# The input stage of a hybrid decoder layer: where the meta tokens' norm runs, and in which order tokens and weights are loaded

## The chip, the cores and the metric

The kernel runs on one core of a Trainium2 chip. A core has a matrix engine (TensorE, PE in the profile), a vector engine (VectorE, DVE), a scalar engine (ScalarE, ACT), GpSimd (POOL) and a sync engine (SyncE, SP). They run side by side and meet through semaphores. SyncE and ScalarE each have a queue from which DMA transfers are issued. The metric is the device time of one execution in microseconds (us); the median over runs is taken.

## The reference

A layer of a decoder trunk in float32, for 1024 tokens of width 1024 with 16 meta tokens put in front. Cut to what matters here:

```python
h = jnp.concatenate([meta, x], axis=1)          # 16 + 1024 tokens
h = layer_norm(h, in_ln_g, in_ln_b)             # the input norm
z = h @ w_in + b_in                             # q | k | v | conv input | gates
a = swa_sink_attention(q, k, v, sinks, ...)     # window 128, 16 meta keys seen by all
c = silu(layer_norm(causal_dwconv(c_val * sigmoid(c_gate), conv_dw, conv_dw_b)))
mixed = sigmoid(g_attn) * (a @ w_attn_proj) + sigmoid(g_conv) * (c @ w_conv_proj)
h = layer_norm(ALPHA * h + mixed @ w_out, ln1_g, ln1_b)
u, g = split(causal_dwconv(h @ ffn_w_up, ffn_dw, ffn_dw_b))
out = layer_norm(ALPHA * h + (gelu(g) * u) @ ffn_w_down, ln2_g, ln2_b)
```

The input norm is `(x - mean) * rsqrt(var + eps) * g + b` for each token; nothing of the big product `h @ w_in` can begin before the first tokens are normed.

## The kernel before, in words

Float32 precision is kept by splitting each operand into a rounded high part and the low rest, and by adding three products (high·high, high·low, low·high) of the faster matmul type. After the input stage the kernel works through the products z, attention and convolution (interleaved), the projections, the FFN's up and down products, and the last norm.

**The input stage.** Tokens come as eight tiles of 128 (`xt[0]` to `xt[7]`) and the meta tokens as one tile `xm`, which holds the 16 tokens twice (partitions 0 to 15 and 16 to 31). Groups of tiles share one norm: group 0 is the meta tile, group 1 is x0 and x1, group 2 is x2, x3 and x4, group 3 is x5, x6 and x7. For each group:

- `stat` (L440, L441): VectorE takes mean and variance of each tile, two halves of 512 and one step that joins them;
- `table` (L464): ScalarE takes the approximate reciprocal square root of the variance;
- `newton` (L470 to L473): VectorE improves it by one Newton step in three operations, and a fourth gives minus mean times root;
- `norm` (L483 on VectorE or L485 on ScalarE): each tile is scaled and shifted, in two halves of 512;
- `turns` (L503): TensorE transposes the normed tiles, eight chunks `k` of 128 features each;
- `scaled` (L509): ScalarE copies the transposed chunk out of PSUM with the norm's gain and offset; `high` and `low` (L516 to L523) split it;
- `z_first` (L557 with the unsplit operands, L560 with the split ones): TensorE's products with the first three weight tiles (k, v and the first q tile).

The first products for tokens 0 to 271 need the meta tile, x0 and x1 together. For chunks 4 to 7 a transposition and a product of L557 take turns on TensorE, with a copy by ScalarE between them.

**What sets the order.** In this stage the order on VectorE, ScalarE and TensorE is the order in which the calls stand from L573 on: the helpers `dv`, `ac` and `pe` chain each instruction to the one before it on its engine. DMA issues have ranks (`with rank(...)`), by which a list scheduler places them. SyncE's queue before is: the meta tokens (twice), x0, x1, the column constants `coll` and `colr`, the first two weight tiles, x2, the third weight tile, x3, x4, x5, x6, x7, a table, the gain rows. A transfer's semaphore is one of eight that are used in turn, so an issue can wait for the eighth transfer before it. After the input stage the scheduler, which plans with its own estimate of times, chooses the order of the instructions of all engines.

At the start, twenty matmuls on a constant (L575) keep TensorE busy until there is something to do. `later` keeps each tile's mean and root for the residual, which is formed long after (L293, L294).

Of the kernel before, what the change touches and what calls it, by code (L numbers as in the profile page):

```python
# [23 lines left out]
F = mybir.dt.float32  # L24
R = mybir.dt.float32r
AF = mybir.ActivationFunctionType
# [3 lines left out]
P = 128  # L30
D = 1024
KC = D // P
NMETA = 16
# [42 lines left out]
RK_TURN, RK_SPLIT, RK_EVAC, RK_START, RK_QKV, RK_RESID, RK_ATT = 450, 500, 600, 1000, 10000, 20000, 30000  # L76
# [36 lines left out]
def tile_hybrid_layer(  # L113
# [3 lines left out]
    nc = tc.nc  # L117
# [5 lines left out]
    def load(o, i):  # L123
        return nc.sync.dma_start(out=o, in_=i)

    def store(o, i):

        return nc.scalar.dma_start(out=o, in_=i)
# [4 lines left out]
    def after(ins, first):  # L133

        tc.add_manual_dep(ins.ins, first.ins.name, mybir.DependencyInfo(
            mybir.DependencyClass.NoSync, mybir.DependencyReason.SCHED_ONLY), reason="order of work")

    @contextmanager
    def rank(p):

        saved = tc.cur_priority
        tc.cur_priority = p
        yield
        tc.cur_priority = saved
# [36 lines left out]
    sp = start.enter_context(tc.tile_pool(name="start", bufs=1, side="right", reuse_waits="tile"))  # L181

    eps = const2.tile([P, 1], F, name="eps")
# [8 lines left out]
    xm = sp.tile([P, D], F, name="xm")  # L192
    with rank(0):
        nc.gpsimd.memset(xm[32:64], 0.0)
        nc.gpsimd.memset(xm[64:96], 0.0)
    with rank(5):
        for i in range(2):
            load(xm[i * NMETA:(i + 1) * NMETA], meta_tokens)
    xt = []

    def load_x(j):
# [98 lines left out]
    def wraw(shape):  # L300
        return wraw_p.tile(shape, F, name="wr", tag="wr")

    def split(raw, hi, lo, behind=None):
        ins = nc.scalar.copy(hi, raw)  # L304
        if behind is not None:
            after(ins, behind)
        return nc.vector.tensor_tensor(lo, raw, f32(hi), OP.subtract)  # L307

    def chunks(t):
        return [t[:, o:o + D].rearrange("p (k c) -> p k c", k=KC) for o in W_AT]  # L310

    def wsp(dtype=R):
        return wsp_p.tile([P, W_LEN], dtype, name="w", tag="w")
# [8 lines left out]
    def weights(shape, fill):  # L322
        fills[0] += 1
        n = fills[0]
        own = n == 3
        raw = OB[:, 0:D].rearrange("p (k c) -> p k c", k=KC) if own else wraw(shape)
        with rank({1: 14, 2: 13, 3: 16, 4: 23}.get(n, RK_SPLIT)):
            last_fill.append(fill(raw))
        hi, lo = chunks(sp.tile([P, W_LEN], R, name="w3") if own else wsp())
        if n <= 3:  # L330
            return hi, lo, raw
        with rank(RK_SPLIT):
            last_split.append(split(raw, hi, lo))
            if n == 7:
                after(last_split[-1], cin_done[-1])
        return hi, lo
# [22 lines left out]
    def z_tile(fill, groups, evac, wt=None):  # L359
        wt = wt or weights([P, KC, P], fill)  # L360
        return [z_group(wt, g, a, b, evac) for g, (a, b) in enumerate(groups)]
# [63 lines left out]
    tokens = [(-1,), (0, 1), (2, 3, 4), (5, 6, 7)]  # L425
    norms, xns, later = {}, {}, []

    def src_of(j):
        return (xt[j], P) if j >= 0 else (xm[:2 * NMETA], 2 * NMETA)

    def stat(t, *js):

        J = len(tokens[t])
        if t not in norms:
            norms[t] = [sp.tile([P, J, 2], F, name=f"mv{t}")] + [sp.tile([P, J], F, name=f"{n}{t}") for n in "trm"]
        for j in js:
            x_, n = src_of(j)
            st_ = small.tile([P, 2, 6], F, name="st")
            for i in range(2):
                dv(V.bn_stats(st_[:n, i], x_[:, i * 512:(i + 1) * 512]))  # L440
            dv(V.bn_aggr(norms[t][0][:n, tokens[t].index(j)], st_[:n].rearrange("p a b -> p (a b)")))  # L441
# [4 lines left out]
        dv(V.tensor_scalar(nsink, sink, -1.0, None, OP.mult))  # L446

    half_st = {}

    def half_stat(t, j, i):  # L450

        if t not in norms:
            norms[t] = [sp.tile([P, len(tokens[t]), 2], F, name=f"mv{t}")] + [
                sp.tile([P, len(tokens[t])], F, name=f"{n}{t}") for n in "trm"]
        if i == 0:
            half_st[j] = small.tile([P, 2, 6], F, name="st")
        dv(V.bn_stats(half_st[j][:, i], xt[j][:, i * 512:(i + 1) * 512]))
        if i == 1:
            dv(V.bn_aggr(norms[t][0][:, tokens[t].index(j)], half_st[j][:, :].rearrange("p a b -> p (a b)")))

    def table(t):
        mv, t_, r_, m_ = norms[t]
        n = src_of(tokens[t][0])[1]
        ac(nc.scalar.activation(r_[:n], mv[:n, :, 1], AF.Abs_reciprocal_sqrt, bias=eps[:n], scale=1.0))  # L464

    def newton(t):
        n = src_of(tokens[t][0])[1]
        mv, t_, r_, m_ = (x_[:n] for x_ in norms[t])
        stt = V.scalar_tensor_tensor
        dv(stt(t_, mv[:, :, 1], EPS, r_, OP.add, OP.mult))  # L470
        dv(stt(t_, t_, -0.5, r_, OP.mult, OP.mult))
        dv(stt(r_, t_, 1.5, r_, OP.add, OP.mult))
        dv(stt(m_, mv[:, :, 0], -1.0, r_, OP.mult, OP.mult))  # L473

    def norm(t, j, on_dve):
        x_, n = src_of(j)
        i = tokens[t].index(j)
        mv, t_, r_, m_ = norms[t]
        xns[j] = sp.tile([P, D], F, name="xn", tag="xn", bufs=4) if j >= 0 else xm
        to = xns[j] if j >= 0 else xm[96:]  # L480
        for a in range(0, D, 512):
            if on_dve:
                dv(V.tensor_scalar(to[:, a:a + 512], x_[:, a:a + 512], r_[:n, i:i + 1], m_[:n, i:i + 1], OP.mult, OP.add))  # L483
            else:
                ac(nc.scalar.activation(to[:, a:a + 512], x_[:, a:a + 512], AF.Identity, bias=m_[:n, i:i + 1],  # L485
                                        scale=r_[:n, i:i + 1]))
        later.append((x_, mv[:n, i, 0:1], r_[:n, i:i + 1], n, j))

    GT = [(-1, 0, 1), (2, 3, 4), (5, 6, 7)]
    turned, tms = {}, {}  # L490
# [34 lines left out]
    def parts(g, *ks):  # L525
        for k in ks:
            high(g, k, on_dve=True)
            low(g, k)

    first = [weights([P, KC, P], in_cols(m)) for m in (4, 5, 0)]  # L530
    evacs0 = [k_evac, v_evac, q_evac(0)]

    def whigh(i):
        ac(nc.scalar.copy(first[i][0], first[i][2]))
# [11 lines left out]
    def z_first(g, tiles, *ks, raw=False):  # L546

        for i in tiles:
            a, b = span(i, g)
            if ks[0] == 0:  # L550
                sums0[i] = pat.tile([P, 512], F, name="ps_z", tag="mm", bufs=3)[:, :b - a]
        for k in ks:
            for i in tiles:
                a, b = span(i, g)
                hi, lo, w = first[i]
                if raw:
                    pe(nc.tensor.matmul(sums0[i], w[:, k], tms[g, k][:, a - HG[g][0]:], start=k == 0, stop=k == KC - 1))  # L557
                    continue
                for j, (w, hl) in enumerate(((lo, 0), (hi, 0), (hi, 1))):
                    ins = nc.tensor.matmul(sums0[i], w[:, k], h0(k, hl, a, b), start=k + j == 0,  # L560
                                           stop=k == KC - 1 and j == 2)
                    if j == 0:
                        pe(ins)
                    pe_done.append(ins)
# [10 lines left out]
        pe(nc.tensor.matmul(warm[:, :P], ones, ones, start=True, stop=True))  # L575
    stat(0, -1)
    table(0)
    stat(1, 0)
    newton(0)
    norm(0, -1, False)  # L580
    stat(1, 1)
    table(1)
    newton(1)
    norm(1, 0, True)
    norm(1, 1, False)
    scales()
    turns(0, 0, 1, 2, 3)
# [10 lines left out]
    evac(0, 0)  # L598
    stat(2, 3)
    stat(2, 4)  # L600
    whigh(1)
    table(2)
    z_first(0, (1,), *range(8), raw=True)
    evac(0, 1)
    newton(2)
# [64 lines left out]

    tc.cur_priority = RK_QKV + 3000
    wt_c1 = weights([P, KC, P], in_cols(11))
    tc.cur_priority = RK_RESID
    for src, mu, rs, n, j in later:
# [19 lines left out]
    bias = ap.tile([P, NH, 272], F, name="bias")  # L694
# [832 lines left out]
    for c in range(FC):  # L1527
        V4, X, Z, Y = (pup.tile([P, 1024], F, name=n, tag=n) for n in ("pw", "px", "pz", "py"))
        passes = ((1,), (0,)) if c == 0 else ((0, 1),)
        for subs in passes:  # L1530
            last = subs == passes[-1]
            w_next = iter(range(7))
            a, b = SUB[subs[0]][0], SUB[subs[-1]][1]
# [314 lines left out]
```

## Time and profile before

| what | us |
|---|---|
| median of 3 runs (range) | 1264.09 (1262.23 to 1264.21) |
| profiled execution, its own time | 1263.24 |
| its span in the trace | 1261.5 |
| TensorE busy, whole span | 1247.8 (99%) |
| VectorE busy | 1076.5 (85%) |
| ScalarE busy | 595.0 (47%) |

How to read the rows in the next section: times count from the start of the span. A row of the timeline has start, busy time, engine, line, operation, `out<-in`, shape and count, and in brackets how long the engine stood idle before it and what ended that. SPq and ACTq are the DMA queues of SyncE and ScalarE. A row of the stretches has, for a stretch of time, its length, each engine's busy time and count of instructions, the granted clock of TensorE (1.00 is full speed), the share of the DMA engines and GB/s. The chain is followed back from the last instruction: each piece is what the next one waited for.

### The profile page before, as it was taken

The numbers are of one execution on the slowest core, as the hardware profiler recorded it, in microseconds if no ns is written. First come the engines' busy times: TensorE is split into PE (matmuls) and PEld (weight loads), VectorE is DVE, ScalarE is ACT, GpSimd is POOL, SyncE is SP. The second block draws the span as 40 slices with busy tenths as digits, with TensorE's granted clock in tenths as the row PEclk, the third lists the DMA queues.
The fourth block names the chain that finished last, engine by engine and source line by source line (L and its number), as shares of the span: only waits on it lengthen the run. The fifth ranks groups of instructions, "written<-read, shape, count | busy, mean of one in ns | idle before, by whom it ended". The sixth has DMA issues, their size and how long they took to land.

```text
span 1261.5 us, 23038 instructions
## 1 busy us (share of the span) xinstructions
PE 1247.8 (99%) x9186; PEld 1181.3 (94%) x9186; DVE 1076.5 (85%) x1858; ACT 595.0 (47%) x1100; POOL 8.0 (1%) x9
## 2 busy tenths in 40 slices
PE   8999999999999999999999999999999999999997
PEld 7999999999999999788999999999999998888886
DVE  7888999999978677448999999998989977996697
ACT  7532345655474233335665555554455544445330
POOL 0000000001000000000000000000000000000000
PEclk9999999999999999999999999999999999999999
DMA  6375543332256564222245546453454567998712
GB/s 254 105 256 145 170 120 97 106 93 85 72 155 169 164 166 124 84 85 82 68 157 196 196 171 216 160 209 135 157 205 165 192 225 252 392 353 329 271 63 84
DMA packets 98701, 212.19 MB, mean 168 GB/s; under 512 B 11411, under 2 KB 38611, under 8 KB 98338
## 3 DMA queue, kind: packets, MB, share of 16 engines
q1 hardware_dynamic: 84474, 199.64, 47.3%
q10 hardware_dynamic: 14120, 11.08, 2.8%
q8 instruction: 72, 1.18, 0.4%
q14 instruction: 35, 0.29, 0.1%
HBM read 150.29 MB, written 62.70 MB: 169 GB/s over the span
## 4 chain that ended last, share of the span: by engine, by line
PE 96%; DVE 2%; ACT 1%; DMA 0%; issue 0%; SPq 0%; DVEq 0%; ACTq 0%
PE px L1549 15%; PE py L1549 10%; PE ps_x L1694 9%; PE ps_z L342 8%; PE ps_z L345 8%; PE ps_z L346 8%; PE ps_z L1694 7%; PE pw L1549 5%; PE pz L1549 5%; PE ps_p L346 2%; PE ps_p L345 2%; PE ps_p L342 2%; PE ps_w L346 2%; PE ps_w L342 2%; PE ps_w L345 2%; PE ps_z L560 2%
## 5 line engine op out<-in xcount | busy, mean ns | idle before, releaser
L342 PE MATMUL ps_z<-RHO,w 128*128 128x256 f32 (+2 forms) x864 | 243.4, 282 | 0.0
L345 PE MATMUL ps_z<-RHO,w 128*128 128x256 f32 (+2 forms) x864 | 242.2, 280 | 0.0
L346 PE MATMUL ps_z<-RHC,w 128*128 128x256 f32 (+2 forms) x864 | 242.2, 280 | 0.0
L342 PEld LDWEIGHTS ps_z<-RHO,w 128*128 128x128 f32 x864 | 162.5, 188 | 1.2 <-ACT FA L709 0.7
L345 PEld LDWEIGHTS ps_z<-RHO,w 128*128 128x128 f32 x864 | 162.5, 188 | 0.5
L346 PEld LDWEIGHTS ps_z<-RHC,w 128*128 128x128 f32 x864 | 162.7, 188 | 0.2
L729 DVE SCALAR_TENSOR_TENSOR FA<-cin,cdw,FA 128x1026 f32<-128x1026 f32 x120 | 154.4, 1297 | 0.7
L1371 DVE TENSOR_TENSOR RHO<-wr,RHO 128x512 fp32r<-128x512 f32 x94 | 64.2, 691 | 7.9 <-ACT RHO L1370 7.9
L304 ACT CAST w<-wr 128x1024 fp32r<-128x1024 f32 x37 | 38.8, 1048 | 63.9 <-PE ps_z L346 45.0
L1370 ACT CAST RHO<-wr 128x512 fp32r<-128x512 f32 x94 | 56.8, 620 | 24.0 <-DVE wr L1388 11.8
L1388 DVE TENSOR_TENSOR wr<-wr 128x512 f32<-128x512 f32 x88 | 60.9, 692 | 0.1
L738 ACT ACTIVATE FA<-ps_z,colr 128x258 f32<-128x258 f32 (+1 forms) x64 | 30.1, 472 | 59.8 <-PE ps_z L346 48.9
L307 DVE TENSOR_TENSOR w<-wr,w 128x1024 fp32r<-128x1024 f32 x37 | 45.1, 1218 | 9.6 <-ACT w L304 9.4
L1561 ACT COPY FA<-px 128x514 f32<-128x514 f32 (+2 forms) x23 | 13.2, 573 | 76.8 <-PE px L1549 76.8
L1371 DVE TENSOR_TENSOR w<-wr,w 128x512 fp32r<-128x512 f32 x60 | 40.9, 691 | 4.8 <-ACT w L1370 4.7
L1549 PE MATMUL px<-OA,RHO 128*128 128x258 f32 x324 | 43.2, 282 | 0.0
L1476 ACT ACTIVATE FA<-OB,coll 128x512 f32<-128x512 f32 x44 | 35.9, 816 | 14.9 <-DVE OB L1557 14.9
L1370 ACT CAST w<-wr 128x512 fp32r<-128x512 f32 x60 | 36.3, 618 | 12.7 <-DMA wr<-in_w_up_dram 5.7
L1561 ACT COPY OB<-px 128x514 f32<-128x514 f32 (+2 forms) x46 | 26.1, 568 | 33.1 <-PE px L1549 33.0
L1549 PE MATMUL px<-OC,RHO 128*128 128x256 f32 x324 | 41.5, 277 | 0.0
L1549 PE MATMUL px<-RHC,RHO 128*128 128x258 f32 (+1 forms) x312 | 41.1, 281 | 0.0
L1549 PEld LDWEIGHTS px<-OA,RHO 128*128 128x128 f32 x324 | 40.5, 189 | 0.2 <-ACT OB L1561 0.2
(451 smaller groups left out, 3302.7 us busy)
## 6 DMA issues: line engine op xcount, KB each, us to landing
wr<-in_w_up_dram SPq DMA_DIRECT2D x44, 512.0 KB, 3.6
wr<-in_w_z_dram SPq DMA_DIRECT2D x29, 512.0 KB, 4.3
OB<-in_w_down_dram SPq DMA_DIRECT2D x24, 512.0 KB, 4.9
fd<-FA SPq DMA_DIRECT2D x44, 256.0 KB, 2.0
FA<-sd SPq DMA_DIRECT2D x15, 512.0 KB, 8.7
qt<-qd SPq DMA_DIRECT2D x28, 256.0 KB, 4.5
OB<-td SPq DMA_DIRECT2D x14, 512.0 KB, 10.0
sgd<-FA ACTq DMA_DIRECT2D x48, 128.0 KB, 3.0
```

Source lines behind the costliest of these rows:

```text
L304: ins = nc.scalar.copy(hi, raw)
L307: return nc.vector.tensor_tensor(lo, raw, f32(hi), OP.subtract)
L342: ins = nc.tensor.matmul(ps, al, bh, start=i == 0, stop=False)
L345: nc.tensor.matmul(ps, ah, bh, start=False, stop=False)
L346: last = nc.tensor.matmul(ps, ah, bl, start=False, stop=i == n - 1)
L729: nc.vector.scalar_tensor_tensor(acc[c], cin[:, j:j + U], wc, acc[c], OP.mult, OP.add)
L1370: nc.scalar.copy(hi, src)
L1371: ins = nc.vector.tensor_tensor(lo, src, f32(hi), OP.subtract)
L1388: ins = nc.vector.tensor_tensor(*x)
L1549: ins = nc.tensor.matmul(o, x[:, ks], bmat(sub, q, hl, k), start=first and k + j == 0, stop=k == 3 and j == 2, skip_group_check=not first)
L1561: copied.append(nc.scalar.copy(*x))
L1694: nc.tensor.matmul(banks[i], l[:, ts], r[:, ws], start=first and a and x + k == 0, stop=z and x == len(ops) - 1 and k == 2, skip_group_che ...
```

## The change

Four things move, all in the first 20 us:

- The two loads of the meta tokens go from SyncE's queue to ScalarE's (`store` issues on ScalarE), with the first rank.
- The order of loads on SyncE becomes: x0, x1, `coll`, `colr`, first weight tile, x2, second weight tile, x3, x4, third weight tile, x5, x6, x7, table, gain rows.
- The meta group's Newton step moves from VectorE (four operations) to ScalarE (seven operations, `newton_act`, with a constant 1.5 in a new tile `c15`). ScalarE's Newton step leaves the root in the tile that was `t`, so the two names are exchanged. The meta tile's norm is cut in two: the first half right after the Newton step, the second behind `table(1)`, the root of group 1.
- `table(2)`, the root of group 2, stands before ScalarE's rounding of the second weight tile (`whigh(1)`) and no longer behind it.

The list of matmuls is the same. In the built program TensorE's order is the same for the first 811 of its 9150 matmuls; then, in the stretch with attention and convolution, the scheduler has another order, and so have VectorE, ScalarE and a few loads there. From the 2648th matmul on TensorE's order is the same again.

```diff
-    with rank(5):
+    with rank(-1):
         for i in range(2):
-            load(xm[i * NMETA:(i + 1) * NMETA], meta_tokens)
+            store(xm[i * NMETA:(i + 1) * NMETA], meta_tokens)
...
-        with rank({1: 14, 2: 13, 3: 16, 4: 23}.get(n, RK_SPLIT)):
+        with rank({1: 13, 2: 16, 3: 19, 4: 23}.get(n, RK_SPLIT)):
             last_fill.append(fill(raw))
...
+    c15 = sp.tile([P, 1], F, name="c15")
+    nc.vector.memset(c15, 1.5)
...
+    def newton_act(t):
+        n = src_of(tokens[t][0])[1]
+        mv, t_, r_, m_ = (x_[:n] for x_ in norms[t])
+        act = lambda *x, **y: ac(nc.scalar.activation(*x, AF.Identity, **y))
+        act(m_, mv[:, :, 0], scale=-1.0)
+        act(t_, mv[:, :, 1], bias=eps[:n], scale=1.0)
+        for i in range(2):
+            act(t_, t_, scale=r_)
+        act(t_, t_, bias=c15[:n], scale=-0.5)
+        act(t_, t_, scale=r_)
+        act(m_, m_, scale=t_)
+        norms[t][1:3] = norms[t][2:0:-1]
+
-    def norm(t, j, on_dve):
+    def norm(t, j, on_dve, halves=(0, 512)):
...
-        for a in range(0, D, 512):
+        for a in halves:
...
     stat(0, -1)
     table(0)
+    newton_act(0)
+    norm(0, -1, False, (0,))
     stat(1, 0)
-    newton(0)
-    norm(0, -1, False)
     stat(1, 1)
     table(1)
+    norm(0, -1, False, (512,))
     newton(1)
...
     stat(2, 3)
     stat(2, 4)
+    table(2)
     whigh(1)
-    table(2)
     z_first(0, (1,), *range(8), raw=True)
```

More of the change, by code (lines that the diff above doesn't have):

```diff
@@ L478, in norm @@
         mv, t_, r_, m_ = norms[t]
-        xns[j] = sp.tile([P, D], F, name="xn", tag="xn", bufs=4) if j >= 0 else xm
+        if halves[0] == 0:
+            xns[j] = sp.tile([P, D], F, name="xn", tag="xn", bufs=4) if j >= 0 else xm
         to = xns[j] if j >= 0 else xm[96:]
-        for a in range(0, D, 512):
+        for a in halves:
             if on_dve:
@@ L486, in norm @@
                                         scale=r_[:n, i:i + 1]))
-        later.append((x_, mv[:n, i, 0:1], r_[:n, i:i + 1], n, j))
+        if halves[-1]:
+            later.append((x_, mv[:n, i, 0:1], r_[:n, i:i + 1], n, j))
     GT = [(-1, 0, 1), (2, 3, 4), (5, 6, 7)]
```

## The prediction

> **What bounds the kernel now.** I read the page first, then the stretches, then the chain up to 23 us, then the timeline of the first 19 us.
>
> ```profile
> span 1261.5 us, 23038 instructions
> PE 96%; DVE 2%; ACT 1%; DMA 0%; issue 0%; SPq 0%; DVEq 0%; ACTq 0%
> ```
>
> TensorE carries 96% of the chain that ends last. The stretches show where it does not run:
>
> ```profile
> 0.00:17.00 17.00, 13.00 (x72) 11.30 (x73) 11.52 (x35) 8.74 (x15) 2.67 (x7) 0.90 0.87 330
> ...
> 150.00:200.00 50.00, 49.87 (x425) 49.56 (x423) 49.78 (x120) 21.20 (x64) 0.00 (x0) 1.00 0.44 124
> 200.00:250.00 50.00, 50.00 (x402) 48.75 (x401) 48.96 (x106) 30.50 (x81) 0.00 (x0) 1.00 0.38 102
> 250.00:300.00 50.00, 49.67 (x404) 48.45 (x403) 48.98 (x101) 24.84 (x66) 5.29 (x2) 1.00 0.34 91
> 300.00:330.00 30.00, 30.00 (x244) 29.33 (x243) 29.72 (x65) 18.14 (x48) 0.00 (x0) 1.00 0.24 71
> 330.00:1240.00 910.00, 909.00 (x6545) 853.09 (x6544) 751.54 (x1228) 430.61 (x710) 0.00 (x0) 1.00 0.52 180
> 1240.00:1262.00 22.00, 13.43 (x60) 10.78 (x58) 17.41 (x39) 1.18 (x4) 0.00 (x0) 0.90 0.25 96
> ```
>
> In each row the second number is TensorE's busy time. It lacks 4.0 us in the first 17 and 8.6 in the last 22, which the change does not touch, and little between. So what the input stage gains reaches the end unshortened, as long as the order between 150 and 330 us, where VectorE too is busy 98 to 100%, stays as good. The whole stake is a few microseconds. The chain through the input stage (start, length, what):
>
> ```profile
> 1.64 3.73 DMA x<-in_x_dram
> ...
> 5.40 1.30 DVE st L440 x2
> ...
> 7.53 1.46 ACT xm L485 x2
> ...
> 9.07 0.30 ACT r L464
> ...
> 10.18 0.56 DVE xn L483
> ...
> 10.78 1.11 PE ps_h L503 x8
> ...
> 12.54 1.27 PE ps_z L557 x2
> 13.82 0.64 PE ps_h L503 x3
> 14.46 0.90 PE ps_z L557 x2
> 15.36 0.33 PE ps_h L503 x3
> 15.69 0.46 PE ps_z L557 x2
> 16.15 0.33 PE ps_h L503 x3
> ...
> 17.26 5.50 PE ps_z L557 x24
> ```
>
> The first transpositions that matter start at 10.78. Ahead of them stand x0's transfer, statistics, the meta Newton step and norm (to 8.99), and only then group 1's root (9.07). A product with its three transpositions takes 0.46 + 0.33 us at the end of the chain but 0.90 + 0.64 earlier, because the clock is halved there (stretches of TensorE alone: length, busy, granted clock, DMA share, GB/s):
>
> ```profile
> 11.50:12.00 0.50, 0.50 (x6) 0.81 1.05 426
> 12.00:12.50 0.50, 0.45 (x3) 0.50 1.06 434
> ...
> 15.00:15.50 0.50, 0.50 (x4) 0.78 1.00 401
> ```
>
> A share of 0.81 is 0.19 us at half clock, so the slice begins at 11.81; 0.78 puts its end at 15.22. It lasts 3.4 us.
>
> **The change part by part.** The rows for it, from the timeline:
>
> ```profile
> 0.73 1.28 ACT L187 ACT_TABLE_LOAD   x1 [0.73 <-PEq L1837]
> 0.74 0.86 SPq L124 DMA_DIRECT2D xm<-in_meta_tokens_dram  x2
> ...
> 1.08 6.58 PE L575 MATMUL ps_w<-ones 128*128 128x128 f32 x40 [1.08 <-DVE ones L241]
> ...
> 3.45 1.27 DVE L440 BATCH_NORM_STATS2 st<-xm 32x6 f32<-32x512 f32 x2 [2.41 <-DMA xm<-in_meta_tokens_dram]
> 4.76 0.20 DVE L441 BATCH_NORM_AGGREGATE mv<-st 32x2 f32<-32x12 f32 x1
> 4.99 0.29 ACT L464 ACTIVATE r<-mv,eps 32x1 f32<-32x1 f32 x1 [2.76 <-DVE mv L441]
> ...
> 8.72 0.21 DVE L441 BATCH_NORM_AGGREGATE mv<-st 128x2 f32<-128x12 f32 x1
> ...
> 11.91 1.29 DVE L440 BATCH_NORM_STATS2 st<-x 128x6 f32<-128x512 f32 x2 [0.49 <-DMA x<-in_x_dram]
> ...
> 17.20 0.21 DVE L441 BATCH_NORM_AGGREGATE mv<-st 128x2 f32<-128x12 f32 x1
> ...
> 18.71 0.30 ACT L464 ACTIVATE r<-mv,eps 128x3 f32<-128x3 f32 x1
> ```
>
> *Loads.* Two issues of together 0.86 us leave SyncE, so x0 is issued at 0.74 and not 1.64. With the same 3.73 us it lands at 4.47; the 128 KB of meta tokens still move beside it, at some 410 GB/s 0.3 us, so 4.5 to 4.8. ScalarE issues the meta loads at the same 0.74, and they should land near 3.45; its table load moves to 1.6 to 2.9, free, since ScalarE has nothing before 4.99. Were the issue to stand behind the table load, the meta tokens would come 1.3 us later; that is the upper end below. [...]
>
> *VectorE.* The four Newton operations leave VectorE. Meta statistics end at 4.96 as before; x0's (1.53 with the joining step, 5.40 to 6.93) then run from 4.98, x1's behind them, and end at 8.04, not 8.93. The new constant is one short fill before 3.45, in idle time.
>
> *ScalarE.* No row shows `newton_act`. Its nearest row is L464, 0.29 us on 32x1, with 0.03 to hand over. From 5.28: two operations that wait for nothing, 0.4, then five that each wait for the last, 5 x 0.32 = 1.6, to 7.3; then half a norm, 0.8 (the two took 1.46), to 8.1. Ends: 0.2 or 0.35 us an operation give 7.6 or 8.3. So group 1's root starts at 8.1, from both sides, against 9.07. VectorE's Newton step and first half norm follow unchanged (9.07 to 10.74), and the transpositions begin at 9.81: **0.97 us earlier**. The second half of the meta norm (0.8) fills ScalarE while VectorE does its Newton step (0.8) and is needed only for chunks 4 to 7; without that cover it would cost x1's norm up to 0.8.
>
> *The chain to 17.26.* The products then start at 11.57. If the half-clock slice stays where it is, the first product does 0.24 us at full clock, and the rest runs at the slow rates: 12.25, 12.89 (turns), 13.79, 14.43, 15.33, then at full clock 15.66, 16.12, 16.45. So 17.26 becomes 16.45: **0.8 us** remain. With no gain from running ahead of the slice it would be 0.5; without a slice it is more (rival one).
>
> *x2 ahead of a weight tile, group 2's root ahead of `whigh(1)`.* At 410 GB/s a 512 KB tile takes 1.28 us, so x2 lands 1.28 + 0.9 earlier than 11.91. Its statistics then start when VectorE is free, near 10.5, and group 2's statistics end near 15.7, not 17.41. But TensorE stands in products until 22.77 (17.26 + 5.50) in any case, so this costs and gains nothing here: the cover is 5.50 us of products. The third weight tile lands about 1.7 us later (two tiles let past, less 0.9), near 15, and is rounded behind group 2's root (18.71 before) and the second tile: hidden. On SyncE every issue waits for the eighth transfer before it; x3 now waits so for x0 (4.8 at the latest), while by the bandwidth it lands two tiles after x2, at 12.3: no loss, and statistics of x3 then no longer wait. Behind ScalarE's two new issues stand only its table load and one warming operation.
>
> *The other order from 150 us on.* Nothing prices it. All of TensorE's idle time there is 0.13 + 0.33 us: the end below. VectorE lacks 2.56 us of being full in the four rows; if the new order doubles that and TensorE waits with it, +2.56: the end above. I take 0, since TensorE's own rows are nearer to it.
>
> Sum, against the profiled execution's own 1263.24: -0.8 gives **1262.4 us**. That execution lies 0.85 below the median of the three runs, so it is 0.13% under the median, inside the 0.2% that a measurement of this kernel can tell from no change.
>
> **The rivals.**
>
> *One: the half-clock slice goes.* TensorE's pause after the filling matmuls (end 7.66) shrinks from 3.1 us to 2.15. Without the slice four pairs of 0.46 + 0.33 take 3.16, from 11.57 to 14.73: 2.5 us less than 17.26, **1260.7 us**. For it: pause and slice are neighbours and the pause is a third shorter. Against: the chain's transpositions already ran for 1 us when the slice began, so some share of idle time, not a pause as such, brings it, and 2.15 of 3.4 us are still idle. [...]
>
> *Two, slower: the new order in the attention stretch makes VectorE wait.* VectorE is full to 0.4 to 2% between 150 and 330 us; idle time there cannot be made up in the stretch. It decides from 4.2 us of new waiting of TensorE (1262.4 to 1266.6, which is the median and 0.2%); at twice VectorE's 2.56 more, 5.1 us, it gives **1267.5 us**, slower by 0.27%. Against: TensorE waited for VectorE only 0.3 us there.
>
> *Three: the gain is not made.* If the five waiting operations on ScalarE average 0.51 us, or if the meta loads stand behind the table load (statistics end at 9.3, root 9.33), group 1's root starts near 9.1 to 9.3 and all stays: **1263.2 us**.
>
> **How the numbers follow.** Forecast (slice stays) 0.45, rival one 0.33, rival two 0.12, rival three 0.10. Low end: 1263.24 - 2.5 - 0.46 = 1260.2. High end: 1262.4 + 2.56 = 1265.0; above it lies rival two. The likeliest case alone is 1261.4 to 1263.5. Faster by over 0.2% (under 1261.56) is rival one: 0.33; within: forecast and rival three, 0.55; slower: 0.12.
>
> **What would show it.** Right: ScalarE's root of group 1 near 8.1 and the first transposition with x0 near 9.8; x2's statistics without a wait; a slice of half clock of 3.4 us; TensorE's idle time from 150 to 330 us under 1 us. Wrong: meta statistics that start after 3.8; seven ScalarE operations that end after 7.7; no slice at all (rival one); new waits of TensorE for VectorE in the attention stretch (rival two).

## The result, and the profile after

The changed kernel takes 1266.33 us (median of 10 runs, 1265.07 to 1267.81); the kernel before, on the same chip, takes 1262.90 (10 runs, 1261.42 to 1264.21). The ratio is 1.0028, with an interval of 1.0019 to 1.0036: slower by 0.28%. Forecast were 1262.4 us, in a range that ends at 1265.0.

The profiled execution of after has an own time of 1266.22 and a span of 1264.3 us; before it was 1263.24 and 1261.5. The chain of after through the input stage (start, length, what):

```profile
0.74 0.42 ACTq L128
...
1.19 5.36 DMA xm<-in_meta_tokens_dram
...
6.65 1.28 DVE st L440 x2
...
8.19 0.29 ACT r L466
...
10.42 0.57 ACT xm L501
11.00 0.26 issue
11.26 0.30 ACT r L466
...
12.37 0.56 DVE xn L499
...
12.97 2.61 PE ps_h L520 x11
...
15.61 1.28 PE ps_z L574 x2
16.89 0.64 PE ps_h L520 x3
17.52 0.91 PE ps_z L574 x2
...
20.83 5.50 PE ps_z L574 x24
```

Before, this chain began with x0's transfer; now it begins with the second load of the meta tokens, issued on ScalarE's queue at 1.19 and landed at 6.55. Everything behind it is in its old order and late: group 1's root at 11.26 and not 9.07, the first transposition with x0 at 12.97 and not 10.78 (2.19 us), and the run of 24 products at 20.83 and not 17.26. So the input stage is 3.57 us slower at the place where 0.8 us less was forecast. The timeline of after has the cause in three rows:

```profile
0.74 0.89 ACTq L128 DMA_DIRECT2D xm<-in_meta_tokens_dram  x2
0.74 0.87 SPq L124 DMA_DIRECT2D x<-in_x_dram  x2
...
6.65 1.27 DVE L440 BATCH_NORM_STATS2 st<-xm 32x6 f32<-32x512 f32 x2 [5.60 <-DMA xm<-in_meta_tokens_dram]
```

The meta loads were issued as early as before, at 0.74, but x0 and x1 were issued beside them. VectorE's first statistics, at 3.45 before, now wait until 6.65. The groups of DMA issues in the first 9 us (KB each, median us from issue to landing), first of before and then of after:

```profile
xm<-in_meta_tokens_dram SPq DMA_DIRECT2D x2, 64.0 KB, 2.2
```

```profile
xm<-in_meta_tokens_dram ACTq DMA_DIRECT2D x2, 64.0 KB, 4.0
```

The 4.0 is that of the first load, which the semaphore records show landed at 4.76; the second took 5.36 us, by the chain's row, to 6.55.

The difference between 2.19 us (transposition) and 3.57 us (products) is the clock. The stretches of after (length, busy time of TensorE, weight loads, VectorE, ScalarE and GpSimd, granted clock, DMA share, GB/s):

```profile
12.00:12.50 0.50, 0.00 (x0) 0.00 (x0) 0.43 (x3) 0.47 (x2) 0.00 (x0) 0.99 1.00 401
12.50:13.00 0.50, 0.03 (x1) 0.03 (x1) 0.50 (x2) 0.50 (x1) 0.00 (x0) 0.50 1.01 401
...
18.50:19.00 0.50, 0.50 (x4) 0.50 (x3) 0.47 (x2) 0.00 (x0) 0.00 (x0) 0.50 0.99 289
19.00:19.50 0.50, 0.50 (x3) 0.35 (x2) 0.20 (x1) 0.39 (x1) 0.00 (x0) 0.69 1.15 459
```

Read as in the prediction, the clock is halved from 12.49 to 19.31 us: 6.8 us, two slices of 3.4, where before had one.

Between the input stage and the end a little came back. In the stretch with attention and convolution:

```profile
150.00:200.00 50.00, 50.00 (x438) 49.84 (x437) 49.81 (x116) 22.34 (x66) 0.00 (x0) 1.00 0.44 127
200.00:250.00 50.00, 50.00 (x403) 48.78 (x402) 48.19 (x104) 28.25 (x72) 0.00 (x0) 1.00 0.42 116
250.00:300.00 50.00, 50.00 (x407) 48.89 (x407) 49.69 (x107) 27.94 (x77) 5.27 (x2) 1.00 0.32 91
300.00:330.00 30.00, 30.00 (x245) 29.22 (x244) 29.69 (x62) 17.29 (x47) 0.00 (x0) 1.00 0.21 67
```

TensorE has no idle time in these rows, where before it had 0.13 + 0.33 us. In the records of single matmuls the delay against before is 3.22 us at 131 us, 2.63 at 353 us and 2.85 at the last matmul. The span grew by 2.8 us and the profiled time by 2.98.

### The profile page after: what moved, and what is told of

Its sections match the earlier page's. It is cut to its first block, busy times and chain, and to the rows that moved or that the text cites. A ratio compares the mean times of both kernels' runs of the same rounds, so it can differ in the third digit from the quotient of the medians.

```text
span 1264.3 us, 23037 instructions
## 1 busy us (share of the span) xinstructions
PE 1249.1 (99%) x9186; PEld 1183.0 (94%) x9186; DVE 1074.1 (85%) x1855; ACT 597.0 (47%) x1107; POOL 7.9 (1%) x9
## 4 chain that ended last, share of the span: by engine, by line
PE 97%; DVE 1%; ACT 1%; DMA 1%; issue 0%; ACTq 0%; DVEq 0%
PE px L1567 15%; PE py L1567 10%; PE ps_x L1712 9%; PE ps_z L342 8%; PE ps_z L345 8%; PE ps_z L346 8%; PE ps_z L1712 7%; PE pz L1567 5%; PE pw L1567 5%; PE ps_p L345 2%; PE ps_p L346 2%; PE ps_p L342 2%; PE ps_w L346 2%; PE ps_w L342 2%; PE ps_w L345 2%; PE ps_z L577 2%
```

## The experiments

Two causes of the late landing were to be told apart (the queue, or what moves beside it), and four candidates for the rest: the Newton step on ScalarE, the load order, the other order in the attention stretch, and the half-clock slice. Each ratio below is to the kernel before, run on the same chip alongside; its median there was 1263.1 to 1263.3 us.

**The meta loads back on SyncE, ahead of x0; all else as in after.**

```diff
-            store(xm[i * NMETA:(i + 1) * NMETA], meta_tokens)
+            load(xm[i * NMETA:(i + 1) * NMETA], meta_tokens)
```

> The changed kernel with one line undone: the meta loads are back on SyncE's queue, ahead of x0. TensorE's order is that of the changed kernel. Theory 'late meta loads' (on ScalarE's queue they land 3.2 us later, and all of the loss comes from that): meta statistics start at 3.45 us again, the transposition that waits for x0 at about 10.2 (10.78 before), and the time is 0.5 to 2 us below the kernel before. Rival 'new order' (the other order of instructions in the attention stretch costs the time): it stays about 3 us above the kernel before.

Measured: 1261.74 us (1260.65 to 1263.91, 11 runs), ratio 0.9989 (0.9981 to 0.9998). From the timeline of this kernel:

```profile
3.44 1.27 DVE L440 BATCH_NORM_STATS2 st<-xm 32x6 f32<-32x512 f32 x2 [2.39 <-DMA xm<-in_meta_tokens_dram]
4.97 0.29 ACT L466 ACTIVATE r<-mv,eps 32x1 f32<-32x1 f32 x1 [2.74 <-DVE mv L441]
7.21 0.81 ACT L501 ACTIVATE xm<-xm,m,t 32x512 f32<-32x512 f32 x1
8.79 0.30 ACT L466 ACTIVATE r<-mv,eps 128x2 f32<-128x2 f32 x1 [0.77 <-DVE mv L441]
10.51 0.33 PE L520 MATMUL ps_h<-coll,xn 128*128 128x128 f32 x1 [1.64 <-DVE xn L499]
```

The meta statistics start at 3.44 again, and with this one word the slower kernel becomes one that is 0.11% ahead of before, by an interval that just excludes no change. TensorE's order is that of after in every matmul, the attention stretch included; so neither that order nor the Newton step on ScalarE made after slow. No half-clock slice is left in this execution, as its stretches show, and the run of 24 products starts at 15.69, 1.57 us ahead of before.

```profile
8.50:12.00 3.50, 1.78 (x15) 1.31 (x13) 2.96 (x13) 2.99 (x5) 0.00 (x0) 1.00 1.02 412
12.00:15.50 3.50, 3.23 (x20) 2.72 (x21) 3.19 (x9) 3.23 (x7) 0.00 (x0) 1.00 1.03 416
```

This profiled execution (1263.91) is the slowest of its runs, so it shows the stage and not the median: it lost the lead again at 143 to 153 us, where the waits of TensorE show a score matmul behind VectorE that the kernel before did not wait for so long:

```profile
PE ps_s L917 <- DVE s L925: 0.8, 1, 0.8
```

**The kernel before with the meta loads on ScalarE's queue, and nothing else.**

```diff
-    with rank(5):
+    with rank(-1):
         for i in range(2):
-            load(xm[i * NMETA:(i + 1) * NMETA], meta_tokens)
+            store(xm[i * NMETA:(i + 1) * NMETA], meta_tokens)
```

> The kernel before with one line changed: the meta loads on ScalarE's queue, first there. Theory 'late meta loads': meta statistics start near 6.6 us, the transposition that waits for x0 near 13.4, time 2.5 to 3.5 us above the kernel before. Rival 'new order' and rival 'Newton step on ScalarE is too slow': no change against the kernel before, within 0.7 us.

Measured: 1266.40 us (1265.84 to 1267.37, 7 runs), ratio 1.0029 (1.0018 to 1.0040). That is the whole loss of after, from one edit:

```profile
6.91 1.27 DVE L440 BATCH_NORM_STATS2 st<-xm 32x6 f32<-32x512 f32 x2 [5.87 <-DMA xm<-in_meta_tokens_dram]
```

**The same queue, but nothing beside it.** In after, every load of SyncE in this stage is held back by a one-column copy from the meta tile into its target, so it can only be issued once the meta tokens are there.

```diff
+    def hold(t):
+        with rank(1):
+            nc.vector.tensor_copy(t[:32, 0:1], xm[:32, 0:1])
+
     def load_x(j):
         t = sp.tile([P, D], F, name=f"x{j}", tag="x", bufs=8)
+        hold(t)
         load(t, x[0, j * P:(j + 1) * P, :])
...
+    hold(coll)
+    hold(colr)
...
+    hold(tab)
...
+    hold(gb[:, 0])
...
+        if n <= 3:
+            hold(raw[:, 0])
```

> The changed kernel, with all loads of SyncE held back until the meta tokens have landed (a one-column copy from the meta tile into each of their tiles comes first). Theory 'shared engines' (the meta loads are late because x0 and x1 move at the same time): alone, they land as on SyncE's queue, and their first reader starts at about 3.4 us. Rival 'slow queue' (ScalarE's queue is slow at the start whatever else moves): the reader starts near 6.6 again. The time itself, some 3 us above the changed kernel, decides nothing.

Measured, in one run: 1264.15 us. The first reader of the meta tokens:

```profile
3.37 0.14 DVE L203 COPY x<-xm 32x1 f32<-32x1 f32 x1 [2.32 <-DMA xm<-in_meta_tokens_dram]
```

and the group of DMA issues in the first 9 us:

```profile
xm<-in_meta_tokens_dram ACTq DMA_DIRECT2D x2, 64.0 KB, 2.1
```

ScalarE's queue is as fast as SyncE's when it is alone: 2.1 us against 2.2 before and 4.0 in after. What delayed the meta tokens was what moved beside them. The time of this kernel was expected some 3 us above after; in its one run it is 2.2 us below, although x0 is issued only at 3.54. With the meta tokens first and x0 behind them, the statistics of both start earlier (4.29 and 7.01) than with both at once (6.65 and 8.08).

The packets in the trace show how. The two meta loads are 16 rows each, one packet of 4 KB for each row. Alone, all 32 packets start between 1.78 and 2.45 us. In after 15 start between 2.44 and 2.89, and the other 17 between 3.98 and 5.66. Before the second group begins, SyncE's queue has started 120 packets of 4 KB, about one x tile of 128 rows. The trace does not name a packet's engine, and these 120 packets are not the whole delay: by the semaphore records 13 of the second load's 16 parts are in by 5.81 us, and the last three come at 6.39 to 6.55. Why these three are later is not shown.

**x0 and x1 cut into four transfers of 32 rows.** If the second group of meta packets waits until a whole x transfer has gone by, smaller transfers ahead let it in sooner.

```diff
-        load(t, x[0, j * P:(j + 1) * P, :])
+        for q in range(0, P, 32 if j < 2 else P):
+            n = 32 if j < 2 else P
+            load(t[q:q + n], x[0, j * P + q:j * P + q + n, :])
```

> The changed kernel with x0 and x1 loaded in four transfers of 32 rows each (2 packets for each DMA engine in place of 8). Theory 'turns by transfer' (between two meta packets of one DMA engine all packets of a whole x transfer go by): the late meta packets come after a quarter of the wait, and the meta statistics start near 4.3 us, not 6.65. Rival 'bytes' (the meta loads wait for the sum of what was issued with them, or for one slow DMA engine): the meta statistics start near 6.6 again. The time itself also pays for six more issues on SyncE and decides nothing.

Measured, in one run: 1268.31 us, and

```profile
5.85 1.27 DVE L442 BATCH_NORM_STATS2 st<-xm 32x6 f32<-32x512 f32 x2 [4.80 <-DMA xm<-in_meta_tokens_dram]
```

Half a hit. The packets did move up: the last of the meta tokens starts at 3.81 and ends at 4.16, not 5.89. But the load is reported as landed only at 5.75, 1.6 us after its last packet; in after that took 0.66 us and alone 0.48. So the statistics gained 0.8 us instead of the 2.3 looked for. What the 1.6 us were spent on is not shown. x0 and x1, in eight transfers, landed later themselves (VectorE waits for them until 9.14 and 11.74; in after they are in at 5.85 and 7.40 by the semaphore records), and the kernel as a whole is slower than after.

**The two good parts, each alone.** First the new load order and the earlier root of group 2, with the meta loads on SyncE and the Newton step on VectorE as before (against the first experiment):

```diff
     table(0)
-    newton_act(0)
-    norm(0, -1, False, (0,))
     stat(1, 0)
+    newton(0)
+    norm(0, -1, False)
     stat(1, 1)
     table(1)
-    norm(0, -1, False, (512,))
```

> The changed kernel with the meta loads on SyncE (as in the first experiment) and with the Newton step and the whole norm of the meta tile as before; what is left of the change is the order of loads and the earlier root of group 2. Theory 'ScalarE's Newton step makes the gain of 1.4 us that the first experiment shows': the transposition that waits for x0 stands at 10.8 as in the kernel before, and the time is that of the kernel before, within 0.7 us. Rival 'the order of loads makes it': 0.7 to 1.5 us below the kernel before.

Measured: 1262.42 us (1261.65 to 1263.92, 10 runs), ratio 0.9997 (0.9988 to 1.0006): no difference that can be told. In the profiled execution (1263.89) the transpositions start at 11.12 and the slice is there. The ten runs fall into two groups, 1261.65 to 1262.48 and 1263.64 to 1263.92, and the mean granted clock of each run tells them apart. In the twelve profiled executions of this case it is 0.998 where the input stage has no slice, 0.997 where it has one of 3.4 us, and 0.995 or 0.996 where it has 6.8 us. Here the four long runs have 0.997 and the six short ones 0.998.

The kernel before is split in the same way. Of its 70 runs beside the experiments, 51 have a clock of 0.997 or less and take 1263.5 us in the mean; 19 have 0.998 or more and take 1262.3. Read so, before itself has the slice in some three of four executions, at a cost of about 1.2 us, and part of every comparison here is how often the slice comes: nine of the first experiment's eleven runs have 0.998 or more.

Then the Newton step on ScalarE and the norm in halves, in the kernel before, its loads untouched:

```diff
     table(0)
+    newton_act(0)
+    norm(0, -1, False, (0,))
     stat(1, 0)
-    newton(0)
-    norm(0, -1, False)
     stat(1, 1)
     table(1)
+    norm(0, -1, False, (512,))
```

> The kernel before with the Newton step of the meta tile on ScalarE and its norm in halves, alone. Theory 'ScalarE's Newton step makes the gain': the transposition that waits for x0 at 10.2 to 10.5 instead of 10.78, group 1's root at about 8.5, time 0.4 to 1.5 us below the kernel before. Rival 'the order of loads makes it': no change, within 0.4 us.

Measured: 1262.17 us (1261.61 to 1262.63, 10 runs), ratio 0.9991 (0.9982 to 1.0000). The timeline of this kernel has every term that the prediction summed for ScalarE:

```profile
5.04 0.29 ACT L466 ACTIVATE r<-mv,eps 32x1 f32<-32x1 f32 x1 [2.81 <-DVE mv L441]
5.24 0.19 ACT L480 ACTIVATE m<-mv 32x1 f32<-32x1 f32 x1
5.34 0.28 ACT L480 ACTIVATE t<-mv,eps 32x1 f32<-32x1 f32 x1
5.65 0.62 ACT L480 ACTIVATE t<-t,r 32x1 f32<-32x1 f32 x2
...
6.96 0.29 ACT L480 ACTIVATE m<-m,t 32x1 f32<-32x1 f32 x1
7.28 0.81 ACT L501 ACTIVATE xm<-xm,m,t 32x512 f32<-32x512 f32 x1
8.31 0.30 ACT L466 ACTIVATE r<-mv,eps 128x2 f32<-128x2 f32 x1 [0.22 <-DVE mv L441]
```

and its stretches show the slice:

```profile
8.50:12.00 3.50, 1.64 (x12) 1.40 (x13) 2.11 (x10) 3.28 (x6) 0.00 (x0) 0.98 1.02 406
12.00:15.50 3.50, 3.50 (x12) 2.77 (x13) 3.06 (x7) 1.98 (x5) 0.00 (x0) 0.53 1.02 415
```

The first transposition comes at 10.02, 0.76 us ahead of before; the run of 24 products at 16.88, only 0.38 ahead, since in this execution the slice stays (11.87 to 15.28). By the granted clock three of the ten runs have it. The profiled execution ends 0.74 us ahead, within what a measurement can tell from no change.

**More filling matmuls.** Three kernels fill TensorE's pause, to see what the half clock costs: the kernel before with 36 in place of 20, the first experiment's with 24, and after with 36 (the cut shows the number for 36).

```diff
-    for i in range(20):
+    for i in range(36):
```

> The kernel before with 36 filling matmuls and not 20 at the start, so that TensorE is busy to about 10.0 us and not 7.66. Theory 'idle time brings the slice of half clock': no slice between 8 and 20 us, products from 12.54 on at 0.46 us each, their 17.26 becomes about 15.7, time 1.5 us below the kernel before. Rival 'the slice has nothing to do with the pause': slice and time as before.

> The first experiment's kernel (all of the change but the meta loads on SyncE) with 24 filling matmuls in place of 20. Theory 'idle time brings the slice of half clock, the input stage's gain reaches the end': no slice, input stage as in the first experiment's profile, time 0 to 0.7 us below that experiment's and 1.4 to 2 us below the kernel before. Rival 'the later order decides': TensorE's order in the attention stretch is another one again, and the time differs from the first experiment's by 1 us or more in either direction with the input stage the same.

> The kernel after with 36 filling matmuls in place of 20, so that TensorE works until 11.3 us and idles only some 1.5 us before the first transposition with x0, which the late meta tokens hold at 12.97 us. Theory (the loss is a later transposition, 2.19 us, and on top a second half-clock slice, some 1.4 us): the slice goes, the transposition stays at 12.9 to 13.1 us, and the z chain runs as in the run with the meta loads back on SyncE (transposition 10.51, 1.58 us ahead of before), so (12.97 - 10.51) - 1.58 = 0.9 us behind before: 1263.9 to 1264.6, against 1266.3. Rival (the clock has no part in it; all of the 3.57 us is waiting): the time stays at 1266 or above. Rival (transpositions do not keep the clock up, so a slice comes in spite of the filling): the clock is 0.5 for 3.4 us from some point after 12 us and the time is about 1265.5.

Before with 36: 1264.76 us (1263.39 to 1267.17, 11 runs), ratio 1.0017 (1.0009 to 1.0026), slower, where 1.5 us less was expected. The slice is gone and the products start at 16.49, 0.77 us early; the filling itself ended only at 11.4 and held the transpositions back by 0.6 us. In the records of single matmuls the lead is still 0.78 us just ahead of 619 us and is lost there, where a product waited for ScalarE, which waited for a weight tile:

```profile
618.98 0.62 ACT L1370 CAST RHO<-wr 128x512 fp32r<-128x512 f32 x1 [1.14 <-DMA wr<-in_w_up_dram]
...
619.92 0.39 PE L1549 MATMUL px<-RHC,RHO 128*128 128x258 f32 x1 [1.23 <-ACT OB L1561]
```

The first experiment's kernel with 24: 1261.76 us (1260.97 to 1263.69, 11 runs), ratio 0.9991 (0.9982 to 1.0000). Products at 15.29, 1.97 us early. Its median is the same as with 20 filling matmuls, which had no slice either in its profiled execution.

After with 36: 1265.78 us (1264.82 to 1267.35, 10 runs), ratio 1.0020 (1.0011 to 1.0030). The stage does what the theory said. The late meta tokens hold the first transposition at 12.96 as in after, but the clock stays full, and the chain reads

```profile
12.96 1.11 PE ps_h L520 x8
...
14.72 0.73 PE ps_z L574 x2
...
18.14 5.50 PE ps_z L574 x24
```

so the products start 0.88 us behind before in place of 3.57. The two slices of after thus cost 2.7 us. The 0.88 that is left is the wait of 2.19 us, less the 1.3 us that before's own slice costs: from the first transposition to the products this kernel and the first experiment's both take 5.18 us, and before takes 6.48. The time, however, is a miss: 1263.9 to 1264.6 was expected. In the records the delay is 0.17 us at 353 us and then grows to 1.77 at the end, by waits that after does not have in this size:

```profile
PE ps_z L1712 <- ACT RHC L1661: 0.6, 1, 0.6
PE px L1567 <- ACT OB L1579: 0.6, 1, 0.6
```

In the profiled executions without a slice the delay against before grows by 0.2 to 1.2 us at 619 us and by 0.4 to 1.2 at 1071; in those with a slice by at most 0.5 and 0.2. Why is not settled. Another order of the matmuls is not the reason: this kernel and the first experiment's with 24 filling matmuls have before's own order on TensorE in every matmul behind the filling. At both places ScalarE waits for a transfer, in the row above for 1.14 us and in this kernel at 1071 us for 0.88.

**The Newton step on ScalarE and 24 filling matmuls, loads as before** (the cut is against the Newton step alone).

```diff
-    for i in range(20):
+    for i in range(24):
```

> The kernel before with the meta tokens' Newton step on ScalarE, the norm in halves and 24 filling matmuls in place of 20; the loads stay as before (meta tokens on SyncE ahead of x0), and the weights' order too. Theory (what gains in this change is the Newton step, and the slice goes with a shorter pause; the load order is worth nothing): root of group 1 near 8.3, transposition near 10.0, no slice of half clock in the first 17 us, 1.9 us ahead of before at the end of the z chain, 1261.3 to 1262.0. Rival (the earlier third tile matters once the slice is gone): 0.5 us or more behind the run that has the new load order and 24 filling matmuls, that is 1262.3 or above.

Measured: 1263.29 us (1262.17 to 1264.14, 10 runs), ratio 0.9999 (0.9989 to 1.0008): the rival's side. The first transposition is at 10.04 and the clock full, so at 22 us the profiled execution, the slowest of the ten, is 2.05 us ahead of before's. By 28.5 us it has given a microsecond back, as the timeline shows:

```profile
12.18 1.29 DVE L440 BATCH_NORM_STATS2 st<-x 128x6 f32<-128x512 f32 x2 [1.51 <-DMA x<-in_x_dram]
...
27.37 0.44 PE L577 MATMUL ps_z<-RHC,w 128*128 128x384 f32 x1 [0.61 <-DVE RHC L540]
```

VectorE waits 1.51 us for x2, its split operands of group 1 come late, and TensorE waits for one. With the new load order and the earlier root of group 2 (the first experiment's kernel with 24) VectorE waits 0.18 us for x2, and TensorE's wait is not there. So these two, worth nothing alone, are worth about a microsecond once the stage ahead of them is 2 us faster.

Another 0.7 us go at 152 us, and in the first experiment 1.6 us at 143 to 153. Both kernels have another order of matmuls than before in that stretch. The first experiment's kernel with 24 filling matmuls has before's order and loses nothing there. So the other order may cost something once the stage is earlier; two executions, each the slowest of its kernel, do not settle it.

The stage in one table (start of the first transposition with x0, state of the clock in the profiled execution, start of the run of 24 products, median; beside the experiments the median of before was 1263.1 to 1263.3):

| kernel | transposition | half clock | products | median us |
|---|---|---|---|---|
| before | 10.78 | 3.4 us | 17.26 | 1262.90 |
| after | 12.97 | 6.8 us | 20.83 | 1266.33 |
| after, meta loads on SyncE | 10.51 | none | 15.69 | 1261.74 |
| the same, 24 filling matmuls | 10.11 | none | 15.29 | 1261.76 |
| before, meta loads on ScalarE | 13.67 | 6.8 us | 20.44 | 1266.40 |
| load order alone | 11.12 | 3.4 us | 17.81 | 1262.42 |
| Newton step alone | 10.02 | 3.4 us | 16.88 | 1262.17 |
| after, 36 filling matmuls | 12.96 | none | 18.14 | 1265.78 |

## Why the prediction was wrong

**The step that failed is *Loads*, in one sentence: "ScalarE issues the meta loads at the same 0.74, and they should land near 3.45".** They landed at 6.55. The prediction priced 128 KB of meta tokens beside x0 by their bytes, 0.3 us, and gave the delay to x0. The bytes were right and their order was not: 120 packets of SyncE's queue, about one x tile, had started before the second group of meta packets, and the last three of the second load's parts came later still, at 6.39 to 6.55. The upper end was bounded by another mechanism, an issue behind the table load, at 1.3 us; the issue did go out at 0.74, and the delay was 3.2 us. A better end stood in the prediction's own numbers: a tile of 512 KB takes 1.28 us, and two of them were issued together with the meta tokens, so 2.6 of the 3.2 us. x0's own gain failed too. Issued at 0.74, it landed at 5.85, not at 4.5 to 4.8, and later than the 5.37 of before.

**The second term is the half-clock slice.** The forecast kept one, rival one dropped it, and after has two, because the pause of TensorE grew from 3.1 us to 5.0 (7.98 to 12.97, but for one transposition) instead of shrinking to 2.15. That slice and pause belong together was right: without the delay the slice is gone in the profiled execution of the first experiment, the products start at 15.69 and the median is 1261.74, between the forecast and rival one's 1260.7. Where this pause is 1.8 us or less, none of the profiled executions has a slice; with 2.3 (Newton step alone) there is one.

But the pause alone does not decide, as the prediction's words on "some share of idle time, not a pause as such" had it, and chance has a part. In each profiled execution the changes of the clock lie whole steps of 3.41 us apart (4.99, 11.81 and 15.22 in before; 5.66, 12.49 and 19.31 in after). Before's half clock follows a step (8.40 to 11.81) in which TensorE worked 1.33 us, that of the Newton step alone a step with 1.54; where there is no slice, the idlest step of the stage has 1.77. Where the steps lie differs from execution to execution. The clock first became full at 4.99 us in before's and at 7.28 in the first experiment's, whose filling so lasted to 8.76 and not 7.66; its pause is 1.1 us shorter by that alone. No run fixed where the steps lie.

*ScalarE* was right. From the root's start the Newton step was priced at 2.3 us (4.99 to 7.3); it took 2.23 in after (8.19 to 10.42) and 2.24 in the Newton step alone (5.04 to 7.28). Group 1's root was to come at 8.1 and came at 8.31 there.

*The chain to 17.26* was right in its kind. With the slice in place, 0.76 us at the transpositions became 0.38 at the products; the prediction had 0.97 become 0.8, with 0.5 as its lower case. A part of the difference is how it read its own lines: the first pair of products took 1.27 us in the chain of before, at half clock, and the working gave it the pace of the later pairs, 0.90. With 1.27 the 0.8 would have been some 0.45.

*x2 ahead of a weight tile and group 2's root* were right as told: load order alone has a ratio of 0.9997. They were hidden, as said, behind the products; in the last experiment, which lacks them, their absence costs a microsecond.

*The other order from 150 us on* was taken as 0, with -0.46 as an end. The delay does fall by 0.59 us there (from 3.22 to 2.63), but in the second experiment, which has before's order in every matmul, it falls by 0.41 too; so 0.2 at most is the order's. Rival two does not explain the result: the order of after is in the first experiment too, and that kernel is not slower than before.

Rival three had the right place, late meta tokens, but it ended where before is, and so did not reach the sign. "Meta statistics that start after 3.8" was the sign of error that came true.

## What to carry to other kernels

Before a small load is moved to another engine's queue, look at what else is issued in the same microsecond: issue it on the same queue ahead of the large ones. A second queue saved 0.9 us of issue here and cost 3.2 us of landing. Price a delay at the head of a stage with what the clock does to the pause that it makes, since 2.2 us of wait became 3.6. An edit that is worth nothing alone can be what the next one needs: the load order cost and gained nothing until the stage before it was 2 us faster. And where the runs of one kernel fall into two groups, look at the granted clock of each run before the profile of one is taken for all.

## What the runs showed of the hardware

Two loads of 64 KB, alone on ScalarE's queue, land 2.1 us after issue; beside two of 512 KB on SyncE's they land after 4.0 and 5.4 us, 17 of their 32 packets behind 120 packets, about one x tile, of the other queue. With those two cut into eight, the second load was reported 1.6 us after its last packet had ended; beside whole tiles this took 0.66 us and alone 0.48.

TensorE was busy with transpositions from 12.97 to 15.58 in after, most of the slice that began at 12.49, and the next slice was halved all the same, while with 36 filling matmuls ahead of the same transpositions the clock was 1.00 from 3.0 to 22.0 us. Whether a transposition holds the clock up like another matmul is not shown: the rows name both MATMUL, and the share of all work fits the clock as well. Inside the slices of the profiled executions, a step of 3.41 us with 2.90 us of work or less (after: 12.49 to 15.90) was followed by another at half clock, and one with 3.10 us or more by full clock (before: 11.81 to 15.22, 3.32 us).
